# Two-layer decoder trunk on one core: a key/query scratch at one stride, and three later due times

## The chip, the cores and the metric

The kernel runs on one core of a Trainium2 chip. The metric is device microseconds of one execution. The time before is the median of three runs. Beside it stands one execution taken by the hardware profiler; all views of the profile below are of that one.

Engines are named as in the profile: PE is TensorE (PEld its weight loads), DVE is VectorE, ACT is ScalarE, POOL is GpSimd, SP is SyncE, which here issues DMAs only. A "q" behind an engine's name (ACTq, SPq) marks work of its instruction queue, DMA issues among it.

## What is computed

Two decoder layers over 1024 tokens of width 1024, all in float32, and a last norm. The parts that matter:

```python
def reference(x, norm1, w_in, b_gate, w_br, w_o, norm2, w_up, conv_w, conv_b, w_down, norm_f):
    for l in range(DEPTH):                                   # DEPTH = 2
        h = rmsnorm(x, norm1[l])
        proj = h @ w_in[l]
        qa, ka, va, qb, kb, vb, gate_pre = jnp.split(proj, splits, axis=-1)
        o_a = dilated_mixture(hd4(qa, DSW_HEADS), hd4(ka, DSW_HEADS), hd4(va, DSW_HEADS))
        o_b = stick_breaking_attention(hd4(qb, SB_HEADS), hd4(kb, SB_HEADS), hd4(vb, SB_HEADS))
        gates = jax.nn.sigmoid(gate_pre + b_gate[l])
        g_a, g_b = gates[..., :D_MODEL], gates[..., D_MODEL:]
        merged = g_a * (o_a @ w_br[l, :OUT_A]) + g_b * (o_b @ w_br[l, OUT_A:])
        x = x + merged @ w_o[l]
        up = rmsnorm(x, norm2[l]) @ w_up[l]
        a, v = up[..., :D_FF], up[..., D_FF:]
        a = causal_depthwise_conv(a, conv_w[l], conv_b[l])
        x = x + (jax.nn.gelu(a, approximate=False) * v) @ w_down[l]
    return rmsnorm(x, norm_f)
```

`dilated_mixture` is a softmax attention with ALiBi of twelve heads in three groups (window 128 at dilation 1, 512 at 4, 2048 at 16), merged by their log-sums. The groups of dilation 4 and 16 attend over tokens taken at stride 4; they are called far below, the first group near. `stick_breaking_attention` has four heads, and its weights hold a running sum over the keys.

## The kernel before

**Products.** Every float32 operand is split in a high and a low fp32r part (`split`: a cast on ACT, L129, and a subtraction on DVE, L130), and a product is three matmuls (high by high, high by low, low by high). Most projection units are a two by two blocked product done with seven block products in place of eight: `pair(...)` computes a first part alone (`ahead`, tile `r_ps`, L155 to L157) and the rest as a "seven" unit (`pair_rest.run`, tiles `i_a`, `i_c`, matmuls L887 to L889). A seven unit needs weight sums: POOL L997 and L999, DVE L1001, POOL L1004, each followed by a split of a weight piece (`w_hi` on ACT, `w_lo` on DVE). Results come back on DVE at L1013, L1018, L1026, L1031 and L1039.

**What sets the order.** PE's order is written out by hand: it is the order in which the Python code emits matmuls. The class `Dense` feeds projection units into attention. Its unit of time is a share, six matmuls of 128x512. `dense.at(n, f)` runs `f` n shares later. While one unit runs, the next is made ready by `ready`, one preparation step (one `yield` ahead of the products) at each turn; a seven unit has READY such steps. The attention items are 16 of the stick-breaking kind (B: scores `z`, a scan L627, `beta` L628, turned by `sb_t` L638), 4 of the near window (N: `p0h`, `p0l`, output L713) and 16 far ones (T, `far_item`: scores z at L584, exponent on ACT L796, turned by PE at L803 to L805, output L813). A T item starts when its key/query piece was fetched six shares ago (LEAD) and when `v1` and `v2`, the value projections of the far groups, are done. DVE, ACT, POOL and SP get their order from a scheduler that goes by priorities and estimated times in the first half of a layer, and each runs its own list strictly in order. DMAs are issued by SP, and some by ACT; every issue takes one of eight completion lanes, and waits if the lane's earlier transfer is not there yet.

**The key/query scratch.** Queries and keys of the far groups come off the projections with heads on partitions, and go through a DRAM scratch `tk` (one for each pair of heads), so that one T item can fetch its pieces as one tile `t_kq`. `pair_kq.put` casts a high part `kq_h` on ACT (L1053 for queries, L1056 for keys), takes a low part on DVE (L1054, L1057), and writes each in pieces of 64 partitions, for each of the two heads (L1062): six DMAs for a query part, four for a key part. High parts are issued by ACT, low ones by SP. `fetch_kq` (L755) reads 128 rows of 6 KB back.

**Values.** `pair_v.put` has a block of values turned by four PE transposes into bank `v_t` (L1074, one of two PSUM banks "s" that scores use as well) two shares after the block is there, and ACT L1078 and DVE L1079 split it for its own scratch. The block comes from DVE L971 (tile `rf`, in `ahead`) or from L1013 to L1039 (tile `u`, in a seven unit).

**Sums of h.** `block_sums` builds the four sums of blocks of h that seven units need (POOL L904 to L906 into `h_sum`, then a split) and spreads them over the shares: `series(after, t, f, lag, gap)` puts one quarter every `gap` steps.

Of the kernel before, what the change touches and what calls it, by code (L numbers as in the profile page):

```python
# [32 lines left out]
PT = 6  # L33
WARM = 6
GROUPS = (2, 2, 3, 4)
READY = 6
ET = mybir.EngineType
IN_ORDER = {ET.PE, ET.Activation, ET.DVE, ET.Pool}
HEAD = 4
# [13 lines left out]
def trunk_kernel(ctx, tc, x, norm1, w_in, b_gate, w_br, w_o, norm2, w_up, conv_w, conv_b, w_down, norm_f, out, depth=None, probe=None):  # L53
# [49 lines left out]
    gs = dr.tile([KD, 2, P, 2, HF], F32, name="gs")  # L103
    gd = dr.tile([NF // 2, 7, P, 2, HF], F32, name="gd")
    obd = dr.tile([P, 2, T], F32, name="obd")
    tk = [dr.tile([2, 4, P, 6, 256], F32, name=f"tk{i}") for i in range(2)]
    tv = [dr.tile([2, 4, P, 2, 256], F32, name=f"tv{i}") for i in range(2)]
    dn = [dr.tile([4, T], F32, name=f"dn{i}") for i in range(2)]
    first_half_product = {}
# [642 lines left out]
    def fetch_kq(i):  # L752

        t = R["kq", i] = sb.tile([P, 6, 256], F32R, tag="xa", bufs=4, name="t_kq")
        nc.sync.dma_start(f32(t), tk[i // 8][i // 4 % 2, i % 4])  # L755

    def fetch_v(i):
        if "vv" not in R:
# [4 lines left out]
    def far_item(dense, pr, s, r, share):  # L763
        i = 8 * pr + 4 * s + r
        slot = 2 * pr + s
        if s == 0 and r == 0:
            R["st1", pr] = sb.tile([P, 2, 2, 2, 4], F32, tag="st1", bufs=2, name="st1")
            R["ot", pr] = None
        st = R["st1", pr]
        shared = {}  # L770

        def score():
            if r == 0:
                bias = share["bias"] = sb.tile([P, 2, 256], F32, tag="bias", name="bias1")
                dve.tensor_scalar(bias[:, 0, :], base0, 4.0 * SLOPES[4 + slot], None, ALU.mult)
                dve.tensor_scalar(bias[:, 1, :], base2, 4.0 * SLOPES[8 + slot], None, ALU.mult)
            bias = share["bias"]
            pt = shared["p"] = sb.tile([P, T], F32, tag="p4", bufs=4, name="p1")
            z0, z1 = bank("s", "z10"), bank("s", "z11")
            t = R["kq", i]  # L780
            for g in range(2):
                scores(z0[:, P * g : P * g + P], t[:, 3 * g + 1, 0:P], t[:, 3 * g + 2, 0:P], t[:, 3 * g, 0:P])
            for g in range(2):
                scores(z1[:, 256 * g : 256 * g + 256], t[:, 3 * g + 1, P:256], t[:, 3 * g + 2, P:256], t[:, 3 * g, :])
            dense.scored = i + 1
            if (s, r) == (1, 0):
                near_stats(pr)
            for n in range(2):
                flat = pt[:, 256:768] if n else pt[:, 0:256]
                if n:  # L790
                    zz, pp, bb = z1, flat, bias.rearrange("p g c -> p (g c)")
                else:
                    zz, pp, bb = z0[:, 0:256].rearrange("p (g c) -> p g c", g=2), flat.rearrange("p (g c) -> p g c", g=2), bias[:, :, P:256]
                nm = st[:, 0, s, n, r : r + 1]
                dve.tensor_tensor_reduce(pp, zz, bb, 1.0, 3e38, ALU.add, ALU.min, nm)
                act.activation(flat, flat, AF.Exp, bias=nm, scale=-1.0, accum_out=st[:, 1, s, n, r : r + 1])  # L796
            if (s, r) == (1, 3):
                factors(pr)

        def turn(g):  # L800
            pt = shared["p"]
            tp = bank("t", "t1")
            pe.transpose(tp[:, 0:P], pt[:, P * g : P * g + P], ident)  # L803
            pe.transpose(tp[:, P : 2 * P], pt[:, 256 + 256 * g : 384 + 256 * g], ident)
            pe.transpose(tp[:, 2 * P : 3 * P], pt[:, 384 + 256 * g : 512 + 256 * g], ident)  # L805
            shared[g] = parts(tp, 384, "p1")

        def apply(g):
            if r % 2 == 0 and g == 0:
                share["o"] = bank("o", "o1")  # L810
            o, oc, vt = share["o"], 256 * (r % 2), R["v", i][:, g]
            for p in (0, 1):
                pe.matmul(o[:, oc : oc + 256], vt[:, 0:P], shared[g][p][:, 0:256], start=(r % 2 == 0 and g == 0 and p == 0), stop=False, skip_group_check=True)  # L813
            for p in (0, 1):
                pe.matmul(o[:, oc + P : oc + 256], vt[:, P:256], shared[g][p][:, 256:384], start=False, stop=(r % 2 == 1 and g == 1 and p == 1), skip_group_check=True)
            if g == 1:
                dense.applied = i + 1
            if r % 2 == 1 and g == 1:
                if R["ot", pr] is None:
                    R["ot", pr] = sb.tile([P, T], F32, tag="ot", name="ot")  # L820
                fold(R["ot", pr][64 * s : 64 * s + 64, 512 * (r // 2) : 512 * (r // 2) + 512], o)
                if s == 1 and r == 3:
                    join(pr)

        return [score], [(lambda g=g: turn(g), lambda g=g: apply(g)) for g in range(2)]
# [67 lines left out]
    def block_sums():  # L893


        keep = {}

        def first(t, a, b, i):
            if i == 0:
                if "r" not in keep:  # L900
                    keep["r"] = quarter("h_sum")
                new_s(t)
            r, (ah, al), (bh, bl) = keep["r"][:, i, :], a()[i], b()[i]
            pool.tensor_tensor(r, f32(al), f32(bl), ALU.subtract)  # L904
            pool.tensor_tensor(r, r, f32(ah), ALU.add)
            pool.tensor_tensor(r, r, f32(bh), ALU.subtract)  # L906

        def further(t, a, i):
            if t == 4:

                S[4] = half(0, 0)
            elif i == 0:
                new_s(t)
            r, (ah, al) = keep["r"][:, i, :], a()[i]
            dve.tensor_tensor(r, f32(ah), r, ALU.subtract)
            dve.tensor_tensor(r, r, f32(al), ALU.add)

        def in_two(t, i):
            split(*S[t][i], keep["r"][:, i, :])

        b11, b12, b21, b22 = (lambda n=n, k=k: half(n, k) for k in range(2) for n in (1, 0))
        todo = []

        def series(after, t, f, lag, gap):

            at = {}
            for i in range(4):
                at.setdefault(i * gap, []).append(lambda i=i: f(i))
                at.setdefault(i * gap + lag, []).append(lambda i=i: in_two(t, i))
            for k in range(3 * gap + lag + 1):  # L930
                todo.append((after, lambda fs=at.get(k, ()): [g() for g in fs]))

        series({"B17"}, 3, lambda i: first(3, b22, b12, i), 6, 4)
        series({"N01s"}, 1, lambda i: first(1, b12, b11, i), 6, 4)
        series({"N11s"}, 2, lambda i: further(2, b22, i), 1, 1)
        series({"plain", "01", "v0"}, 4, lambda i: further(4, b21, i), 1, 1)
        return todo

    def zeros():

        none = sb.tile([P, 4, 256], F32, tag="ot", name="none")
        pool.memset(none[0:64], 0.0)
        for pr in range(2):
            for g in range(2):
                for s in range(2):
                    nc.sync.dma_start(tk[pr][s, :, 64:128, 3 * g + 2, :].rearrange("r p c -> p r c"), none[0:64])

    def pair(dense, l, offs, tiled, put):

# [27 lines left out]
    def pair_rest(dense, l, offs, put, view, grid, kept):  # L977
# [10 lines left out]
        def run():  # L988
# [8 lines left out]
            pool.tensor_tensor(u2, a11, a21, ALU.subtract)  # L997
            yield
            pool.tensor_tensor(a21, a21, a22, ALU.add)  # L999
            yield  # L1000
            dve.tensor_tensor(a11, a21, a11, ALU.subtract)  # L1001
            w6 = piece(a11)
# [42 lines left out]
    def pair_kq(dense, l, g, pr):  # L1045
        off = 256 * g + P * pr

        def put(c, n, x, psum):
            hi = small("kq_h", F32R)
            lo = small("kq_l", F32R) if psum else x.bitcast(F32R)  # L1050
            hv, lv, xv = (t if t is x and psum else t.rearrange("p (r j) -> p r j", r=4) for t in (hi, lo, x))
            if c:
                act.mul(hv, xv, -SCALE)  # L1053
                dve.scalar_tensor_tensor(lv, xv, -SCALE, f32(hv), ALU.mult, ALU.subtract)  # L1054
            else:
                act.copy(hv, xv)  # L1056
                dve.tensor_tensor(lv, xv, f32(hv), ALU.subtract)  # L1057
            for s in range(2):
                rows = slice(64 * s, 64 * s + 64)
                for src, kind, up in ((hv, c, 0), (hv, 1, 64), (lv, 2, 0)) if c else ((hv, 0, 0), (lv, 0, 64)):  # L1060
                    there = tk[pr][s, :, up : up + 64, 3 * (g - 1) + kind, n * P : (n + 1) * P]
                    (nc.sync if src is lv else act).dma_start(there.rearrange("r p j -> p r j"), f32(src[rows]))  # L1062
            if (c, n) == (1, 1):
                dense.done.add(f"{g}{pr}")

# [2 lines left out]
    def pair_v(dense, l, g):  # L1068
# [17 lines left out]
        def put(c, n, x, psum):  # L1086
            f = x
            if psum:
                f = small("vf")
                act.copy(f.rearrange("p (r j) -> p r j", r=4), x)  # L1090
            dense.at(2, lambda: turn(c, n, f))

        off = OFF_VA + 256 * g
        return pair(dense, l, (off, off + P), True, put)
# [763 lines left out]
```

## Time and profile before

| | |
|---|---|
| median of three runs | 2773.81 us (2773.45 to 2774.67) |
| the profiled execution | 2779.93 us, of which the span of instructions is 2778.1 us |
| mean granted TensorE clock of it | 0.989 |
| busy in it: PE, PEld | 2688.1 us (97%), 2241.6 us (81%) |
| DVE, ACT, POOL | 2091.8 us (75%), 1327.2 us (48%), 695.2 us (25%) |
| moved in it | 449.92 MB, 162 GB/s |
| key/query scratch writes: of high parts from ACT | 96 of 128 KB, 3.6 us to landing |
| of low parts from SP | 64 of 128 KB, 3.4 and 3.7 us |
| key/query fetches from SP | 32 of 768 KB, 5.3 us |

In the profile's table of groups, a row has the line, the engine, the operation and its tiles, then busy time, then the idle time of the engine just before these instructions and what ended it. In the table of waits, a row says which engine waited before which tile's instruction for whom, the sum in us, how often, and the longest. In a timeline, a row has the start in us, the duration, the engine and line, and in brackets how long the engine was idle before it and what ended that. Two matmuls of 128x512 at full clock begin 0.23 us apart, though each lasts 0.39 us: they overlap.

### The profile page before, as it was taken

Reading aid. Unit: us, or ns where it says so; the run is one execution under the profiler, and the core shown is the slowest. Engines: PE = TensorE matmul, PEld = TensorE weight load, DVE = VectorE, ACT = ScalarE, POOL = GpSimd, SP = SyncE. Lnnn points to the kernel's source line nnn. Section 1 sums busy time; section 2 is a strip of 40 time slices with the busy share of each in tenths; the row PEclk is TensorE's granted clock in tenths of the full one; section 3 lists DMA queues with packets and bytes.
Section 4 is the critical chain, followed back from the end, with each engine's and each line's share of the span. In section 5 each row is a group of like instructions: output and inputs, shape, how many; then the busy total and the mean of one; then the engine's idle time right before and its main releaser. Section 6 shows DMA issues by size and latency. Waiting matters only on the chain. (4 is left out here: it accounts for less than half of the span.)

```text
span 2778.1 us, 37044 instructions
## 1 busy us (share of the span) xinstructions
PE 2688.1 (97%) x13098; PEld 2241.6 (81%) x13098; DVE 2091.8 (75%) x3132; ACT 1327.2 (48%) x2458; POOL 695.2 (25%) x509
## 2 busy tenths in 40 slices
PE   8998999999999999999999989999999999999999
PEld 8877877888888888888888778778788888888888
DVE  5877865676688888897657767556757889988965
ACT  5655633346455555532335655343544555554225
POOL 1004121213224343421110041222222334443210
PEclk9999999999999999999999989999999999999999
DMA  5023378555324434588401234876632344446863
GB/s 149 27 80 110 115 208 247 190 192 180 99 96 155 159 138 158 195 330 315 168 32 47 78 99 134 232 233 198 227 119 83 123 158 167 138 154 238 327 257 122
DMA packets 394630, 449.92 MB, mean 162 GB/s; under 512 B 22748, under 2 KB 315980, under 8 KB 392908
## 3 DMA queue, kind: packets, MB, share of 16 engines
q1 hardware_dynamic: 368332, 434.96, 47.1%
q10 hardware_dynamic: 26112, 12.59, 1.7%
q8 instruction: 104, 1.70, 0.3%
q14 instruction: 82, 0.67, 0.1%
HBM read 300.61 MB, written 146.87 MB: 161 GB/s over the span
## 5 line engine op out<-in xcount | busy, mean ns | idle before, releaser
L130 DVE TENSOR_TENSOR w_lo<-up_a,w_hi 128x512 fp32r<-128x512 f32 x240 | 236.8, 993 | 20.0 <-ACT w_hi L129 20.0
L129 ACT CAST w_hi<-up_a 128x512 fp32r<-128x512 f32 x240 | 149.4, 622 | 184.1 <-PE u_a L888 45.8
L1614 DVE TENSOR_TENSOR x<-x,d_ps 128x512 f32<-128x512 f32 (+1 forms) x228 | 152.0, 672 | 77.4 <-PE d_ps L1608 76.1
L1345 POOL TENSOR_TENSOR cv<-cv 128x512 f32<-128x512 f32 x88 | 131.8, 1508 | 249.6 <-DVE cv L1340 139.7
L129 ACT CAST w_hi<-w_raw 128x512 fp32r<-128x512 f32 x176 | 109.1, 621 | 145.0 <-PE o_ps L156 67.2
L130 DVE TENSOR_TENSOR w_lo<-w_raw,w_hi 128x512 fp32r<-128x512 f32 x176 | 127.2, 726 | 64.9 <-ACT w_hi L129 64.1
L130 DVE TENSOR_TENSOR g<-cv,g 128x512 fp32r<-128x512 f32 x154 | 151.7, 986 | 5.2 <-ACT g L129 2.8
L129 ACT CAST w_hi<-in_a 128x512 fp32r<-128x512 f32 x112 | 68.8, 617 | 136.2 <-PE i_a L888 66.1
L1606 PE MATMUL d_ps<-gd_in,w_hi 128*128 128x512 f32 (+1 forms) x340 | 130.3, 383 | 1.7 <-issue 0.9
L1608 PE MATMUL d_ps<-gd_in,w_lo 128*128 128x512 f32 (+1 forms) x340 | 129.8, 382 | 0.0
L1607 PE MATMUL d_ps<-gd_in,w_hi 128*128 128x512 f32 (+1 forms) x340 | 129.8, 382 | 0.0
L997 POOL TENSOR_TENSOR u<-in_a 128x512 f32<-128x512 f32 x28 | 37.3, 1332 | 355.3 <-DVE w_lo L130 88.1
L887 PE MATMUL u_a<-hh,w_hi 128*128 128x512 f32 x320 | 124.7, 390 | 0.3 <-DVE u L1496 0.2
L889 PE MATMUL u_a<-hh,w_lo 128*128 128x512 f32 x320 | 124.5, 389 | 0.0
L888 PE MATMUL u_a<-hl,w_hi 128*128 128x512 f32 x320 | 124.5, 389 | 0.0
L887 PE MATMUL u_a<-t_hi,w_hi 128*128 128x512 f32 x320 | 124.5, 389 | 0.0
L888 PE MATMUL u_a<-t_lo,w_hi 128*128 128x512 f32 x320 | 124.5, 389 | 0.0
L889 PE MATMUL u_a<-t_hi,w_lo 128*128 128x512 f32 x320 | 124.5, 389 | 0.0
L1606 PE MATMUL d_ps<-gd_in,wd 128*128 128x512 f32 (+1 forms) x292 | 113.9, 390 | 0.0
L129 ACT CAST g<-cv 128x512 fp32r<-128x512 f32 x154 | 94.9, 616 | 37.6 <-POOL cv L1345 29.2
L1608 PE MATMUL d_ps<-gd_in,wd 128*128 128x512 f32 (+1 forms) x292 | 112.8, 386 | 0.0
L1607 PE MATMUL d_ps<-gd_in,wd 128*128 128x512 f32 (+1 forms) x292 | 112.7, 386 | 0.0
(390 smaller groups left out, 8739.0 us busy)
## 6 DMA issues: line engine op xcount, KB each, us to landing
gd<-g SPq DMA_DIRECT2D x154, 512.0 KB, 3.6
gd_in<-gd SPq DMA_DIRECT2D x154, 512.0 KB, 6.5
up_a<-in_w_up_dram SPq DMA_DIRECT2D x80, 512.0 KB, 5.5
in_a<-in_w_in_dram SPq DMA_DIRECT2D x56, 512.0 KB, 5.0
w_raw<-in_w_in_dram SPq DMA_DIRECT2D x104, 256.0 KB, 3.0
t_kq<-tk SPq DMA_DIRECT2D x32, 768.0 KB, 5.3
wd_raw<-in_w_down_dram SPq DMA_DIRECT2D x22, 1024.0 KB, 7.9
gin<-gs SPq DMA_DIRECT2D x32, 512.0 KB, 4.3
```

The costliest lines, as they stand in the source:

```text
L129: act.copy(hi, src)
L130: dve.tensor_tensor(lo, src, f32(hi), ALU.subtract)
L887: pe.matmul(o, w[0][:, c], rh, start=(first and i == 0), stop=False, skip_group_check=True)
L888: pe.matmul(o, w[0][:, c], rl, start=False, stop=False, skip_group_check=True)
L889: pe.matmul(o, w[1][:, c], rh, start=False, stop=(last and i == 3), skip_group_check=True)
L997: pool.tensor_tensor(u2, a11, a21, ALU.subtract)
L1345: return lambda: pool.tensor_tensor(dst, a, b, ALU.subtract)
L1606: pe.matmul(o[:, sub], wh[:, c], gh[:, sub], start=(i == 0 and k in (0, 4, 5)), stop=False, skip_group_check=True)
L1607: pe.matmul(o[:, sub], wh[:, c], gl[:, sub], start=False, stop=False, skip_group_check=True)
L1608: pe.matmul(o[:, sub], wl[:, c], gh[:, sub], start=False, stop=(i == m - 1), skip_group_check=True)
L1614: dve.tensor_tensor(x, x, o[:, sub], ALU.add)
```

## The change

Four edits.

1. The scratch `tk` holds both heads' rows under one another, 128 rows of twelve 1 KB slots for each residue of the stride (six for each group: zeros, query low, query high, key high, key low, one unused). Query and key parts are written once, as one DMA of 128 partitions (256 KB) each for the high and the low part, both issued by SP. Over both layers 160 writes become 64, and ACT issues none of them. The zeros that fill the lower half of an operand are one slot per group, written once for both heads. A T item fetches with two DMAs in place of one: 64 partitions of two runs of 3 KB, and 64 partitions of six runs of 1 KB. The scores read the same operands from other slots.
2. READY goes from 6 to 7, with one empty step between POOL L999 and DVE L1001.
3. Values are turned four shares after their block, not two.
4. The first two series of `block_sums` put a quarter every five steps, not four.

```diff
-READY = 6
+READY = 7
...
-    tk = [dr.tile([2, 4, P, 6, 256], F32, name=f"tk{i}") for i in range(2)]
+    tk = [dr.tile([4, P, 12, 256], F32, name=f"tk{i}") for i in range(2)]
...
     def fetch_kq(i):
         t = R["kq", i] = sb.tile([P, 6, 256], F32R, tag="xa", bufs=4, name="t_kq")
-        nc.sync.dma_start(f32(t), tk[i // 8][i // 4 % 2, i % 4])
+        there = tk[i // 8][i % 4, 64 * (i // 4 % 2) : 64 * (i // 4 % 2) + 64]
+        nc.sync.dma_start(f32(t[0:64]).rearrange("p (g k) c -> p g (k c)", g=2), there.rearrange("p (g k) c -> p g (k c)", g=2)[:, :, 256:1024])
+        nc.sync.dma_start(f32(t[64:128]), there.rearrange("p (k b) c -> p k b c", b=2)[:, :, 0, :])
...
-        series({"B17"}, 3, lambda i: first(3, b22, b12, i), 6, 4)
-        series({"N01s"}, 1, lambda i: first(1, b12, b11, i), 6, 4)
+        series({"B17"}, 3, lambda i: first(3, b22, b12, i), 6, 5)
+        series({"N01s"}, 1, lambda i: first(1, b12, b11, i), 6, 5)
...
     def zeros():
-        pool.memset(none[0:64], 0.0)
+        pool.memset(none, 0.0)
         for pr in range(2):
             for g in range(2):
-                for s in range(2):
-                    nc.sync.dma_start(tk[pr][s, :, 64:128, 3 * g + 2, :].rearrange("r p c -> p r c"), none[0:64])
+                nc.sync.dma_start(tk[pr][:, :, 6 * g, :].rearrange("r p c -> p r c"), none)
...
             pool.tensor_tensor(a21, a21, a22, ALU.add)
+            yield
             yield
             dve.tensor_tensor(a11, a21, a11, ALU.subtract)
...
-            for s in range(2):
-                rows = slice(64 * s, 64 * s + 64)
-                for src, kind, up in ((hv, c, 0), (hv, 1, 64), (lv, 2, 0)) if c else ((hv, 0, 0), (lv, 0, 64)):
-                    there = tk[pr][s, :, up : up + 64, 3 * (g - 1) + kind, n * P : (n + 1) * P]
-                    (nc.sync if src is lv else act).dma_start(there.rearrange("r p j -> p r j"), f32(src[rows]))
+            for src, kind in ((hv, 2), (lv, 1)) if c else ((hv, 3), (lv, 4)):
+                there = tk[pr][:, :, 6 * (g - 1) + kind, n * P : (n + 1) * P]
+                nc.sync.dma_start(there.rearrange("r p j -> p r j"), f32(src))
...
-            dense.at(2, lambda: turn(c, n, f))
+            dense.at(4, lambda: turn(c, n, f))
```

Three places show how instructions move. The first is PE, in the stick-breaking stretch of the first layer, at the first value turn. Before:

```order
L155 MATMUL r_ps<-hh_362,w_hi 128x512
L156 MATMUL r_ps<-hl_363,w_hi 128x512
L157 MATMUL r_ps<-hh_362,w_lo 128x512
L1074 MATMUL v_t<-ident,rf 128x128 x4
L584 MATMUL z<-kt,qt 128x512
L585 MATMUL z<-kt,ql 128x512
```

Now, from those scores on:

```order
L584 MATMUL z<-kt,qt 128x512
L585 MATMUL z<-kt,ql 128x512
L155 MATMUL r_ps<-hh_362,w_hi 128x512
L156 MATMUL r_ps<-hl_363,w_hi 128x512
L157 MATMUL r_ps<-hh_362,w_lo 128x512
L649 MATMUL sb_o<-sbh,vb 128x256
L638 MATMUL sb_t<-ident,beta 128x128 x3
L156 MATMUL r_ps<-hl_363,w_hi 128x512
L157 MATMUL r_ps<-hh_362,w_lo 128x512
L1074 MATMUL v_t<-ident,rf 128x128 x4
L649 MATMUL sb_o<-sbh,vb 128x256
```

The turn `v_t` now stands behind twelve more matmuls of the projection (two shares; rows that repeat are left out), and with them behind two pairs of scores, a piece of the stick-breaking output and a turn of `beta`.

The second place is ACT, at the end of the last key/query unit of a layer, where the second pair of T items of a head pair begins (`p` is the tile of far scores, `st` its statistics, lines after the change are two higher). Before:

```order
L1056 CAST kq_h<-u 128x512
L129 CAST w_hi<-u 128x512
L1062 DMA tk_91<-kq_h 64x4x128 x2
L1053 ACTIVATE kq_h<-u 128x512
L129 CAST w_hi<-in_a 128x512
L1062 DMA tk_91<-kq_h 64x4x128 x4
L796 ACTIVATE p_4452,st_4221<-p_4452,st_4221 128x256
L796 ACTIVATE p_4452,st_4221<-p_4452,st_4221 128x512
```

Now:

```order
L129 CAST w_hi<-u 128x512
L1058 CAST kq_h<-u 128x512
L599 COPY fold<-o_4297 64x512
L129 CAST w_hi<-in_a 128x512
L1055 ACTIVATE kq_h<-u 128x512
L129 CAST w_hi<-in_a 128x512
L798 ACTIVATE p_4427,st_4206<-p_4427,st_4206 128x256
L798 ACTIVATE p_4427,st_4206<-p_4427,st_4206 128x512
```

The six DMA rows between the casts and the exponents are gone.

The third place is DVE, in a value unit of the first layer, around the weight difference L1001 (L1003 after the change) and the results L1018 and L1026 (L1020 and L1028). Before:

```order
L1013 TENSOR_TENSOR u<-u,i_a 128x512
L130 TENSOR_TENSOR w_lo<-in_a,w_hi 128x512
L1018 TENSOR_TENSOR u_3964<-u,i_c 128x512
L130 TENSOR_TENSOR w_lo<-in_a,w_hi 128x512
L1001 TENSOR_TENSOR in_a<-in_a 128x512
L1026 TENSOR_TENSOR u_3964<-u_3964,i_a 128x512
```

Now:

```order
L1015 TENSOR_TENSOR u<-u,i_a 128x512
L130 TENSOR_TENSOR w_lo<-in_a,w_hi 128x512
L1020 TENSOR_TENSOR u_3932<-u,i_c 128x512
L1003 TENSOR_TENSOR in_a<-in_a 128x512
L130 TENSOR_TENSOR w_lo<-in_a,w_hi 128x512
L1028 TENSOR_TENSOR u_3932<-u_3932,i_a 128x512
```

The weight difference still stands ahead of L1028; a low part that stood ahead of it now stands behind it.

More of the change, by code (lines that the diff above doesn't have):

```diff
@@ L781, in score @@
             for g in range(2):
-                scores(z0[:, P * g : P * g + P], t[:, 3 * g + 1, 0:P], t[:, 3 * g + 2, 0:P], t[:, 3 * g, 0:P])
+                scores(z0[:, P * g : P * g + P], t[:, 3 * g + 1, 0:P], t[:, 3 * g, 0:P], t[:, 3 * g + 2, 0:P])
             for g in range(2):
-                scores(z1[:, 256 * g : 256 * g + 256], t[:, 3 * g + 1, P:256], t[:, 3 * g + 2, P:256], t[:, 3 * g, :])
+                scores(z1[:, 256 * g : 256 * g + 256], t[:, 3 * g + 1, P:256], t[:, 3 * g, P:256], t[:, 3 * g + 2, :])
             dense.scored = i + 1
```

## The prediction

> **What bounds the kernel now.** I read the page's busy table first, then the windows of 50 us, then who PE waits for.
>
> ```profile
> span 2778.1 us, 37044 instructions
> PE 2688.1 (97%) x13098; PEld 2241.6 (81%) x13098; DVE 2091.8 (75%) x3132; ACT 1327.2 (48%) x2458; POOL 695.2 (25%) x509
> 250.00:300.00 50.00, 43.59 (x213) 35.97 (x212) 35.79 (x63) 27.09 (x59) 31.23 (x23) 0.90 0.29 91
> 400.00:450.00 50.00, 45.12 (x216) 36.03 (x216) 31.02 (x63) 18.65 (x39) 9.39 (x7) 0.97 0.91 256
> 1600.00:1650.00 50.00, 44.01 (x222) 36.88 (x223) 31.35 (x64) 24.93 (x61) 27.26 (x21) 0.88 0.30 97
> ```
>
> PE is the bound: 2688.1 of 2778.1 us. The change takes no matmul away, so it can win only from the 90 us in which PE stands, and from the clock: in the windows (PE's busy time is first, the granted clock third from the end) a stretch with stops has a clock of 0.88 to 0.97. Both losses sit in the attention part of each layer. The table of waits says whom PE waits for:
>
> ```profile
> PE sb_t L638 <- DVE beta L628: 10.8, 12, 2.2
> PE o L713 <- ACT p0h L129: 6.4, 2, 3.2
> PE o L813 <- ACT p1h L129: 5.4, 5, 1.6
> PE v_t L1074 <- DVE rf L971: 5.3, 2, 2.7
> PE t L803 <- ACT p L796: 5.2, 3, 2.2
> PE v_t L1074 <- DVE u L1026: 5.1, 2, 3.0
> PE o L813 <- DVE p1l L130: 4.7, 10, 1.1
> PE z L584 <- DVE st L795: 4.3, 4, 1.8
> PE i_a L887 <- ACT w_hi L129: 2.6, 2, 1.6
> PE t L804 <- ACT p L796: 1.8, 5, 0.4
> PE i_a L887 <- DVE u L1031: 1.5, 2, 0.8
> ```
>
> Three are close to the change: both value turns (5.3 and 5.1 us) and the far probabilities `p` (5.2 and 1.8). A stop costs more than itself, as the first value turn in PE's timeline shows, with DVE's rows below:
>
> ```profile
> 221.67 0.39 PE L156 MATMUL r_ps<-hl,w_hi 128*128 128x512 f32 x1
> 221.90 0.40 PE L157 MATMUL r_ps<-hh,w_lo 128*128 128x512 f32 x1
> 224.97 0.63 PE L1074 MATMUL v_t<-ident,rf 128*128 128x128 f32 x4 [2.67 <-DVE rf L971]
> 227.24 0.53 PE L584 MATMUL z<-kt,qt 128*128 128x512 f32 x1 [1.18 <-ACT stay L625]
> 228.00 0.63 PE L155 MATMUL r_ps<-hh,w_hi 128*128 128x512 f32 x1
> 228.43 0.63 PE L156 MATMUL r_ps<-hl,w_hi 128*128 128x512 f32 x1
> 223.14 1.09 DVE L628 TENSOR_TENSOR beta<-beta,stay 128x895 f32<-128x895 f32 x1
> 224.15 0.68 DVE L971 TENSOR_TENSOR rf<-q1s,r_ps 128x512 f32<-128x512 f32 x1
> ```
>
> Ahead of the stop matmuls begin 0.23 us apart, behind it 0.43: half speed, for some seven of them, so 7 x 0.20 = 1.4 us lost on top of the wait. I take 1.4 us for each stop that is removed or made.
>
> **The change part by part.**
>
> *Value turns two shares later, first place* (`v_t` from `rf`, once a layer). Removed: the wait, 5.3 us in both layers; the wait behind it (1.18, in both layers 2.4), since `v_t` takes one of the two banks that `z` needs; two slow stretches, 2.8. Together 10.5. After the change PE goes on at 222.13 with the four scores (0.9), two shares (2.8), outputs and turn (0.8), so it reaches `v_t` at about 226.6; `rf` is done at 224.83. Late next is `sb_t`, which needs `beta` (done at 224.23): PE would be there at 222.13 + 0.9 + 1.4 + 0.5 = 224.9, so with 0.7 us to spare. The bank is still shared, and `v_t` now stands close ahead of the next scores: I allow 2 us of new waits a layer for it and credit **6.5 us** (bounds 0 and 10.5).
>
> *Value turns, second place* (`v_t` from `u` of L1026, once a layer), and *ACT without DMA issues*. These belong together; the rows are ACT, POOL, DVE and PE around the last key/query unit ahead of the values:
>
> ```profile
> 390.40 4.41 ACTq L1062 DMA_DIRECT2D tk<-kq_h  x4
> 394.85 0.62 ACT L129 CAST w_hi<-in_a 128x512 fp32r<-128x512 f32 x1 [3.97 <-DMA tk<-kq_h]
> 396.38 1.28 POOL L997 TENSOR_TENSOR u<-in_a 128x512 f32<-128x512 f32 x1 [10.08 <-DVE w_lo L130]
> 397.74 1.26 POOL L999 TENSOR_TENSOR in_a<-in_a 128x512 f32<-128x512 f32 x1
> 399.03 0.69 DVE L1001 TENSOR_TENSOR in_a<-in_a 128x512 f32<-128x512 f32 x1 [2.83 <-POOL in_a L999]
> 399.64 0.68 DVE L1026 TENSOR_TENSOR u<-u,i_a 128x512 f32<-128x512 f32 x1
> 400.38 0.66 PE L1074 MATMUL v_t<-ident,u 128*128 128x128 f32 x4 [3.02 <-DVE u L1026]
> ```
>
> One chain: four issues hold ACT's queue for 4.41 us, the cast `w_hi` starts when they are through, its low part releases POOL L997, L999 follows, L1001 waits for it, and L1026, which is ready, stands behind L1001. Moving the turn alone gains one share, not two: the fifth product accumulates in the bank that L1026 reads, and begins one share behind the turn's old place. So alone it gives 2 x 1.4 = 2.8. With the issues off ACT the chain starts up to 4 us earlier, and the rest of the 3.0 goes too. All of it is 5.1 + 2.8 of slow clock = 7.9; I credit **6.5** (bounds 2.8 and 7.9).
>
> *Far exponents behind ACT's issues.*
>
> ```profile
> 447.09 0.69 DVE L795 CUSTOM_DVE_ANT_0 p<-z,bias 128x512 f32<-128x512 f32 x1
> 447.52 3.97 ACTq L1062 DMA_DIRECT2D tk<-kq_h  x4
> 451.55 0.51 ACT L796 ACTIVATE p<-p,st 128x256 f32<-128x256 f32 x1 [3.54 <-issue]
> 452.20 0.33 PE L803 MATMUL t<-ident,p 128*128 128x128 f32 x1 [2.23 <-ACT p L796]
> ```
>
> `p` is there at 447.78, ACT comes to it at 451.55: the 3.97 us of four issues lie between, and nothing else. Without them the exponents (some 1.2 us) end by 449.1; PE asked for them at 452.20 - 2.23 = 449.97. So the waits for `p` go: 5.2 + 1.8 in the table, plus 1.4 for each layer's long one, 9.8. I credit **8** (bounds 5 and 9.8), since DVE's rows of L795 may come later in a new order.
>
> *The prepared weight piece* (`i_a` for `w_hi` and for L1031, 2.6 + 1.5 = 4.1): the same chain over POOL L997, whose tile comes free when scratch writes have landed. Credit **2.5** (bounds 0 and 4.1). *Scores behind statistics* (`z` for L795, 4.3): only their two at key/query units are touched; credit **1** (bounds 0 and 3.6).
>
> *Weight difference later, READY 7.* In the listed order L1001 still stands ahead of L1026, with one `w_lo` less ahead of it. In feed-forward units the extra step is empty. I credit nothing; if L1001 stays the head of DVE's list at the wrong time, the price is that of the chain above, inside its bounds. *Sums of h five steps apart*: POOL's list is the same and so is ACT's around it; nothing. The wait it could have touched, `o` for `p0h` (6.4), stays, and so does most of `beta` (10.8).
>
> *The DMAs.*
>
> ```profile
> t_kq<-tk SPq DMA_DIRECT2D x32, 768.0 KB, 5.3
> DMA to landing us min/median/max: 4.2/5.3/10.9
> tk<-kq_h ACTq DMA_DIRECT2D x96, 128.0 KB, 3.6
> 427.14 0.56 SPq L755 DMA_DIRECT2D t_kq<-tk  x1
> 444.35 0.22 PE L584 MATMUL z<-t_kq 128*128 128x128 f32 x1
> ```
>
> (The second row is of those fetches.) SP keeps its 64 scratch writes; one of each pair now waits for ACT's cast, which comes ahead of the low part that the other waits for, so SP's list waits for nothing later than before. It gains 32 fetches. A fetch is asked for 17.2 us ahead of its use and lands after 5.3: 11.9 us of cover, and even twice 5.3 costs nothing. The issues themselves, 32 of 0.56 us, are 18 us over both layers on an engine that does nothing else.
>
> The row above has ACT held for 4.41 us by four issues, about 1.1 us each, where SP's took 0.56. [...] The trace shows ACT, not SP, as the queue that holds up PE.
>
> *New waits.* `v1` and `v2` are done two shares later, so all 32 far items start later against the dense work and meet other neighbours. Their waits now (5.4 + 4.7 + 4.3 = 14.4 us) are 0.45 an item. I allow four new stops of 1.4 us each, slow clock or wait, that is **-5.5** (bounds 0 and -15, where every item waits twice as long as now).
>
> Sum: 6.5 + 6.5 + 8 + 2.5 + 1 - 5.5 = **19 us**. The profiled execution took 2779.93 us (its span and 1.8 around it), which becomes 2761; it stands 6.1 above the median of 2773.81, which becomes **2755 us**.
>
> **The rivals.**
>
> *The stops only move* (no change). Each waiting instruction still has its chain behind DVE, at 75% busy; the far items start elsewhere. For it: the row of `o` for `p1l`, ten small waits that have nothing to do with the change. Against it: ACT is 48% busy and the 4 us of issues have no second cause. It would need new waits of 19 to 30 us against credits of 24.5: 2768 to 2779; I take 2772.
>
> *The split fetch comes late* (slower). Half of each fetch now comes in 1 KB runs, 384 of them, and the fetches of the first items of a layer go out while the DMA engines are busy for 0.91 of the time (window 400 to 450). The worst fetch took 10.9 us with its 6 KB runs. If a small run costs so much that such a fetch takes twice that, 21.8, it is 4.6 us past its use; it decides from 17.2 us on. Four such items a layer are 8 x 4.6 = 37 us, more than the credits of 24.5: 2786. Behind a late fetch the next DMAs of SP's list wait as well, since completion lanes are handed on in turn. Against it: the median of 5.3, and 4 MB less written at that very time.
>
> *The clock doesn't come back with the gaps.* If half speed comes from something else than the stop ahead of it, six stops give back 6 x 1.4 = 8.4 us less: 10.6 in place of 19, 2763. The rows at 221.90 to 228.43 speak against it. [...]
>
> *The edit doesn't do what it says.* For the weight difference and the sums of h the listed order says so already; it is in the sum at nothing.
>
> *All of it gains*: 10.5 + 7.9 + 9.8 + 4.1 + 3.6 = 36 and no new wait: 2738.
>
> **How the numbers follow.** My forecast, with part of the credits: 0.52. The clock stays: 0.08. All of it gains: 0.13. The stops only move: 0.15, of which a third is still faster by more than the bound below. The split fetch late: 0.12. The range runs from 2736, just past the full gain, to 2771; beyond it lie the slower rival and half of the case of no change, about 0.2 together. Without the far cases the forecast's own range is 2745 to 2764. What a measurement of this kernel can tell from no change is about 0.2%, 5.5 us: faster means under 2768.3, slower over 2779.4. Faster 0.52 + 0.08 + 0.13 + 0.05 = 0.78, same 0.1, slower 0.12.
>
> **What would show it.** In the changed profile the rows of ACTq with `tk` are gone, and `t` for `p` falls from 7.0 us in two rows to under 1.5. `v_t` for `rf` and for L1026 are gone or under 1 us together. ACT's wait for DMA `tk` ahead of `w_hi` is gone. The clock rises from 0.989 to about 0.993. `o` for `p0h` stays at 6.4. The prediction is wrong if PE's sum of stops stays near 90 us, with new rows that name a fetch `t_kq`, a load of `in_a` or `z` behind `v_t`.

## The result, and the profile after

| | before | changed |
|---|---|---|
| median | 2773.63 us (4 runs, 2772.07 to 2774.67) | 2749.56 us (4 runs, 2745.2 to 2750.43) |
| ratio | | 0.9911, 95% interval 0.9893 to 0.9928 |
| profiled execution, its span | 2779.93, 2778.1 us | 2750.43, 2748.6 us |
| clock | 0.989 | 0.993 |

The kernel became 24 us faster; 19 were forecast, inside the range. Beside the experiments below the changed kernel ran once more, with a median of 2748.78 us and a ratio of 0.9906 (0.9892 to 0.9921).

The page and rows of PE's table of waits of the changed kernel (who waits for whom, total us, times, longest; rows on which no reading rests are left out):

```profile
span 2748.6 us, 36975 instructions
PE 2672.8 (97%) x13098; PEld 2232.0 (81%) x13098; DVE 2096.1 (76%) x3132; ACT 1328.1 (48%) x2458; POOL 694.2 (25%) x509
PE sb_t L638 <- DVE beta L628: 14.5, 12, 2.2
PE z L584 <- DVE st L797: 8.0, 11, 1.3
PE o L713 <- ACT p0h L129: 6.4, 2, 3.2
PE o L815 <- DVE p1l L130: 6.1, 7, 1.8
PE br_ps L155 <- ACT br_w L129: 3.1, 1, 3.1
PE br_ps L157 <- DVE br_w L130: 2.3, 1, 2.3
PE z L584 <- ACT stay L625: 2.1, 3, 1.2
PE i_a L889 <- DVE u L1028: 1.4, 2, 1.2
PE o L815 <- ACT p1h L129: 0.5, 2, 0.3
```

Both rows of `v_t` are gone, and so are both rows of `t` waiting for ACT's `p` (5.2 and 1.8 us before). The wait of `z` for `stay` behind the first value turn fell from 4.5 to 2.1, and `o` for `p1h` from 5.4 to 0.5. The other signs that the prediction named are there too: the clock is 0.993, `o` for `p0h` stays at 6.4, and the span without PE's busy time is 75.8 us in place of 90.0. PE's busy time fell by 2688.1 - 2672.8 = 15.3 us with the same 13098 matmuls. Most of it is the clock: of the 29.5 us between the two profiled executions about half is standing time and half is matmuls that took less time, up to 13.7 us of it by the count of slow spans below. The stops in the timelines sum to 82.3 us before and 68.2 now. The trace's record of the granted clock has PE, up to its last matmul, at half clock for 61.4 us before (18 spans of 3.41 us, in 15 stretches) and 34.1 us now (10 spans, in 7 stretches). An estimate from these: with matmuls 0.43 us apart in place of 0.23, a span that is worked through loses at most half of itself, 1.7 us, so eight spans fewer are worth up to 13.7 us.

New or longer are `sb_t` for `beta` (10.8 to 14.5), `z` for L797 (4.3 to 8.0), `o` for `p1l` (4.7 to 6.1), and two waits for `br_w`, 5.4 us together (1.4 before).

Where the time came from can be read by taking the same dense matmul (the k-th of tile `r_ps`, or of `i_a` and `i_c`) in both timelines and subtracting its start. The steps of that difference, in us (first and second layer; negative is earlier now):

| stretch | first | second |
|---|---|---|
| stick-breaking items, with the first value turn | -4.2 | -3.5 |
| near items | -0.1 | -1.5 |
| key/query units up to the second value turn | -2.6 | -3.0 |
| across the second value turn | -3.9 | -4.0 |
| far items | -4.9 | -6.3 |
| branch projections behind them | +1.3 | +5.4 |

These sum to -27.3; 1.9 more lie at the program's start, where input transposes wait for no cause that the profile shows, and the feed-forward parts give 0.5. The profiled execution before stood 6 us above its median, the one after 1, so the medians differ by 5 us less.

The rows that answer to the first value turn, of the changed kernel (PE, then DVE):

```profile
222.65 0.60 PE L1074 MATMUL v_t<-ident,rf 128*128 128x128 f32 x4
227.68 0.90 PE L638 MATMUL sb_t<-ident,beta 128*128 128x128 f32 x3 [2.00 <-DVE beta L628]
223.16 2.29 DVE L627 TENSOR_TENSOR_SCAN stay<-stay,zero 128x1024 f32<-128x1024 f32 x1 [1.15 <-ACT stay L625]
226.41 1.22 DVE L628 TENSOR_TENSOR beta<-beta,stay 128x1023 f32<-128x1023 f32 x1
```

The turn itself no longer waits. PE now comes sooner to the next `sb_t` and waits 2.0 us there for the last and longest scan (2.29 us) and the `beta` behind it.

Second value turn and far exponents (PE, ACT, PE):

```profile
391.14 0.47 PE L889 MATMUL i_a<-hh,w_hi 128*128 128x512 f32 x1 [1.23 <-DVE u L1028]
392.61 0.60 PE L1074 MATMUL v_t<-ident,u 128*128 128x128 f32 x4
410.64 0.63 ACT L1055 ACTIVATE kq_h<-u 128x512 fp32r<-128x512 f32 x1 [0.27 <-DVE u L1041]
412.38 0.51 ACT L798 ACTIVATE p<-p,st 128x256 f32<-128x256 f32 x1 [1.11 <-DVE st L797]
414.31 0.27 PE L805 MATMUL t<-ident,p 128*128 128x128 f32 x1
```

As worked out, `i_a` now stands in front of the turn and waits for the bank that L1028 (L1026 before) reads: 1.23 us here, 0.16 in the second layer, in place of 3.02 and 2.10. Between the cast `kq_h` and the exponent ACT waits only for DVE's statistics (1.11 us), where four issues stood before, and PE's turn of `p` comes without a wait.

The transfers of the scratch in the changed kernel, and one row of experiment 3 (KB each, median us to landing):

```profile
t_kq<-tk SPq DMA_DIRECT2D x64, 384.0 KB, 6.9
tk<-kq_h SPq DMA_DIRECT2D x32, 256.0 KB, 2.4
tk<-u SPq DMA_DIRECT2D x24, 256.0 KB, 3.2
...
tk<-kq_h SPq DMA_DIRECT2D x96, 128.0 KB, 2.5
```

A write of 256 KB over 128 partitions lands in 2.4 to 3.2 us, one of 128 KB over 64 took 3.4 to 3.7. The shape is not shown to be the reason: in experiment 3, where SP issues all the old pieces, these land in 2.5 us too (last row). Half a fetch takes 6.9, where the whole took 5.3. No wait of PE's scores is put down to `t_kq`.

### The profile page after: what moved, and what is told of

Same layout as the page of the kernel before. It is cut to its first block, busy times and chain, and to the rows that moved or that the text cites. A ratio compares the mean times of both kernels' runs of the same rounds, so it can differ in the third digit from the quotient of the medians.

```text
span 2748.6 us, 36975 instructions
## 1 busy us (share of the span) xinstructions
PE 2672.8 (97%) x13098; PEld 2232.0 (81%) x13098; DVE 2096.1 (76%) x3132; ACT 1328.1 (48%) x2458; POOL 694.2 (25%) x509
```

## The experiments

All ratios are against the kernel before on the same chip; intervals are 95%.

**1. The scratch edit alone.** The `tk`, `fetch_kq`, `zeros` and `put` parts of the diff; the rest as before.

> Only the scratch edit of the change; value turns after two shares, READY 6 and gap 4 as before. My theory: the gain from ACT's freed queue is in this edit, that is 8 (far exponents) + 2.5 + 1 + the part of the second value turn that hangs on ACT's cast (7.9 - 2.8 = 5): 12 to 17 us faster than before, 2757 to 2762. Rival, the later value turns carry the change and the far items' new place does the rest: at most 5 us faster. In the trace PE's wait t for ACT p goes in my theory, and the first value turn's wait for rf (5.3 us) stays.

2753.54 us (2752.81 to 2757.67), ratio 0.9928 (0.9915 to 0.9941): 20 us faster, more than I allowed for. In its table of waits the `p` rows are gone, and the value turns are still there:

```profile
PE v_t L1073 <- DVE rf L972: 4.8, 2, 2.4
PE v_t L1073 <- DVE u L1027: 3.9, 2, 2.5
```

The scratch edit carries most of the change. The second turn's wait fell only from 5.1 to 3.9, so not the part I had put down to ACT's cast, but the far items, made the surplus over my sum. Taken matmul by matmul as above, the two layers gain 2.8 us at the second turn, 5.0 in the key/query units and 15.2 at the far items, where my sum had 5, 2.5 and 9.

**2. The value turns alone.**

```diff
-            dense.at(2, lambda: turn(c, n, f))
+            dense.at(4, lambda: turn(c, n, f))
```

> Only the value turns at four shares; scratch, READY and gap as before. My theory: 6.5 for the turn of rf and 2.8 for that of u, less new waits of the far items, which now begin later: 3 to 9 us faster, 2765 to 2771; ACT's four issues still hold up the far exponents somewhere. Rival, the turns carry the change: 15 us or more. Second rival, the stops only move: within 2 us of before.

2767.97 us (2764.15 to 2770.91, 11 runs), ratio 0.9977 (0.9968 to 0.9985): 6 us faster, as my theory had it. The stop for `p` is still there, in one of 3.2 us a layer, and `sb_t` has the same new wait as in the changed kernel:

```profile
PE sb_t L638 <- DVE beta L628: 14.2, 14, 2.2
PE t L803 <- ACT p L796: 6.4, 2, 3.2
```

**3. Issues off ACT, in the old pieces.**

```diff
-                    (nc.sync if src is lv else act).dma_start(there.rearrange("r p j -> p r j"), f32(src[rows]))
+                    nc.sync.dma_start(there.rearrange("r p j -> p r j"), f32(src[rows]))
```

> The kernel before with one word changed: the high parts' writes, in their old pieces, are issued by SP too (160 small writes, all on SP). My theory, it is ACT's queue that costs: 8 to 15 us faster than before, 2759 to 2766, a little less than the scratch edit alone since SP's list is longer by 96 issues. Rival, it is the number of writes and their landing (POOL's tiles come free late): within 3 us of before. Second rival, SP becomes the head of line: slower than before.

2771.83 us (2766.43 to 2775.41, 12 runs), ratio 0.9990 (0.9981 to 0.9998): 2 us. My theory fell, as it was put: freeing ACT is not enough. The trace shows what takes its place (SP, POOL, DVE, PE in the first layer):

```profile
417.30 4.98 SPq L1062 DMA_DIRECT2D tk<-kq_h  x2
434.12 0.32 SPq L996 DMA_DIRECT2D u<-q  x1
434.29 1.29 POOL L997 TENSOR_TENSOR u<-in_a 128x512 f32<-128x512 f32 x1 [21.06 <-DMA tk<-u]
436.99 0.69 DVE L1001 TENSOR_TENSOR in_a<-in_a 128x512 f32<-128x512 f32 x1 [1.51 <-POOL in_a L999]
441.85 0.41 DVE L795 CUSTOM_DVE_ANT_1 p<-z,bias 128x256 f32<-128x256 f32 x1
442.32 0.48 PE L584 MATMUL z<-t_kq 128*128 128x128 f32 x1 [3.92 <-DVE st L795]
```

From 417.3 to 432 SP issues nothing but small scratch writes. The load of the next unit's `u` comes behind them at 434.12, POOL starts on that unit's tile at 434.29, the weight difference and its splits follow on DVE, the statistics L795 stand behind these, and PE waits 3.92 us for them. So the stop for `p` has become a stop of `z` for L795 (10.0 us in the run, 4.3 before): SP became the head of line.

**4. Few writes, but the high parts from ACT.** The changed kernel with one line back:

```diff
-                nc.sync.dma_start(there.rearrange("r p j -> p r j"), f32(src))
+                (nc.sync if src is lv else act).dma_start(there.rearrange("r p j -> p r j"), f32(src))
```

> The changed kernel, with the 32 writes of the high parts (256 KB, 128 partitions) issued by ACT again; all else as changed (2750 us). Theory A, it takes both to be few and off ACT's queue, and each issue from ACT still waits for a completion lane in front of casts: 2 to 6 us slower than the changed kernel, 2752 to 2756. Theory B, only the number of writes matters (moving 160 small ones to SP alone gave 2 us): within 2 us of it. Theory C, any issue from ACT costs as much as the four did: 8 us or more slower.

2753.84 us (2751.45 to 2755.32), ratio 0.9927 (0.9914 to 0.9939): 4 to 5 us slower than the changed kernel (2749.56 and 2748.78), theory A in size, though the intervals of the ratios overlap. On the same chip ran the changed kernel without its empty step (experiment 5, 2747.28 to 2749.23): all five runs here (2751.45 and up) lie above all four there. Its trace (ACT, then PE):

```profile
1790.01 0.62 ACT L1058 CAST kq_h<-u 128x512 fp32r<-128x512 f32 x1 [5.21 <-DMA tk<-kq_h]
1790.66 0.37 ACTq L1062 DMA_DIRECT2D tk<-kq_h  x1
1795.94 0.33 PE L584 MATMUL z<-t_kq 128*128 128x128 f32 x1 [4.22 <-DVE st L797]
```

An issue from ACT takes 0.37 us here (the old pieces' took 0.64 by their median), so it is not the issuing that costs. A cast stood still for 5.21 us until an earlier scratch write had landed, and PE then waited 4.22 us. By these two runs most of the scratch edit's 20 us comes with the merged writes. The issuing engine is worth 2 us with the old pieces and 4 to 5 with the merged ones. What it is in the merging that pays, the number of writes, their width, the 4 MB less that are moved or the split fetch, no run here separates.

**5. READY 7 and the empty step alone, and left out.** Alone on the kernel before:

> Only READY 7 and the empty step ahead of the weight difference. My theory: nothing, within 3 us of before, since the difference still stands ahead of the same result in DVE's list. Rival: that result comes off the head-of-line wait and the second value turn's wait goes: 5 to 8 us faster.

2772.97 us (2768.71 to 2777.34, 11 runs), ratio 0.9995 (0.9987 to 1.0004): nothing. Left out of the changed kernel (READY 6, one `yield` less):

> The changed kernel with READY 6 and without the empty step ahead of the weight difference. My theory, the step does nothing: within 2 us of the changed kernel's 2750. Rival, it keeps the weight difference off the head of VectorE's list once the rest is in place: 4 us or more slower, with waits of i_a for L1026 and for w_hi.

2748.94 us (2747.28 to 2749.23), ratio 0.9908 (0.9895 to 0.9922): nothing either.

**6. The sums of h at gap 4 in the changed kernel.**

> The changed kernel with the sums of h at gap 4, as before. My theory, the gap does nothing: within 2 us of the changed kernel's 2750. Rival, it spares the near window's waits: 3 us or more slower, with the wait of o for p0h over 6.4 us.

2745.47 us (2744.46 to 2746.63), ratio 0.9897 (0.9884 to 0.9911). This hinted at 3 to 4 us that the wider gap costs, though its waits were the same as the changed kernel's (`p0h` 6.4 in both). So I left both small edits out together, beside the changed kernel on one chip:

> Only the scratch edit and the value turns at four shares: READY 6 and gap 4 as before. My theory, the other two edits do nothing: within 2 us of the changed kernel on the same chip. Rival, the wider gap costs 4 us, as the run without it hinted (2745.5): 3 us or more faster than the changed kernel.

> The changed kernel itself once more, beside the three below on the same chip, so that they are compared with it there. Expected 2747 to 2751.

2748.69 us (2747.86 to 2749.82) against 2748.78 (2744.96 to 2751.54): the same. So the two edits together do nothing. Whether gap 4 with READY 7 is really 3 us faster stays open: its four runs lie below the four of experiment 5's second kernel on the same chip, but the intervals of the ratios overlap, and it was not run again.

**7. The value turns at two shares in the changed kernel.**

> The changed kernel with the value turns at two shares again (all other edits in). My theory, the first place's wait for rf (2.4 and 2.4 us, with slow clock and the bank's 1.2 behind it) comes back and the new wait of sb_t for beta goes: 3 to 7 us slower than the changed kernel, close to the scratch edit alone (2753.5). Rival, the turns' gain of 6 us alone is gone once ACT's queue is free: within 2 us of the changed kernel.

2751.1 us (2748.83 to 2752.76), ratio 0.9915 (0.9900 to 0.9930), against 0.9906 (0.9892 to 0.9921) for the changed kernel on the same chip: 2.3 us, not clear of the spread, nearer the rival than my theory. The waits of the turns come back, and others go:

```profile
PE sb_t L638 <- DVE beta L628: 10.5, 10, 2.2
PE v_t L1074 <- DVE rf L972: 4.8, 2, 2.4
PE o L815 <- DVE p1l L130: 3.3, 6, 1.1
PE v_t L1074 <- DVE u L1028: 2.8, 2, 1.4
```

`sb_t` is back at 10.5, `o` for `p1l` at 3.3, `z` for L797 at 2.9, and `br_w` waits 1.4. Against these, `o` for `p1h` is back at 4.3 and `z` for `stay` at 4.5. On top of the scratch edit, turning values two shares later takes 7.6 us of waits off the turns and 6 off `p1h` and `stay`, and gives it back at the other four places: the stops sum to 65.7 us here and to 65.9 in the changed kernel's second profile. On other chips the scratch edit alone and with the turns (experiment 6) have ratios 6 us apart, so 2 to 6 us is what these runs show of the turns' worth there.

**8. The value turns at three shares in the changed kernel.**

> The changed kernel with the value turns at three shares. By the chain at the first place: rf is done some 0.4 us after PE gets there, and the turn stands ahead of sb_t, so that beta's new wait of 2.0 us shrinks by the turn's place and no more: within 3 us of the changed kernel, 2745 to 2752. Rival, three is as bad as two: 2753.

2741.77 us (2739.76 to 2743.71), ratio 0.9880 (0.9863 to 0.9896): 7 us faster than the changed kernel on the same chip, past what I expected, and the best of all kernels here. The intervals of the two ratios just touch (0.9896 and 0.9892), and no run of the one lies among the runs of the other.

```profile
PE sb_t L638 <- DVE beta L628: 12.5, 12, 2.2
PE z L584 <- DVE st L797: 5.2, 11, 1.3
PE br_ps L155 <- DVE gin L1259: 4.1, 3, 2.7
PE o L815 <- DVE p1l L130: 1.3, 5, 0.4
```

The turns wait no longer, as at four, but the far items begin only one share later, and `o` for `p1l` falls from 6.1 to 1.3. Matmul by matmul, the far items of both layers together gain 15 us, where they gained 11 in the changed kernel. The branch projections of the second layer lose 4 us here too, now for `gin` (2.7 us at once). What the wait for `p1l` was in the changed kernel can be read from POOL, DVE and PE in the first layer:

```profile
439.07 1.28 POOL L998 TENSOR_TENSOR u<-in_a 128x512 f32<-128x512 f32 x1 [12.32 <-DMA tk<-u]
441.74 0.69 DVE L1003 TENSOR_TENSOR in_a<-in_a 128x512 f32<-128x512 f32 x1 [4.26 <-POOL in_a L1000]
442.35 0.55 DVE L130 TENSOR_TENSOR p1l<-t,p1h 128x384 fp32r<-128x384 f32 x1
442.95 0.39 PE L815 MATMUL o<-p1l,t_v 128*128 128x256 f32 x1 [1.79 <-DVE p1l L130]
```

The weight difference L1003, the very one that was asked for later, is the head of DVE's list for 4.26 us until POOL is through, and the low part of the far probabilities stands behind it. This is one of seven such waits, and that its going makes the 4 us is an argument from the rows, not tried by itself.

**9. The splits of the sums asked for later.** The changed kernel with

```diff
-        series({"B17"}, 3, lambda i: first(3, b22, b12, i), 6, 5)
-        series({"N01s"}, 1, lambda i: first(1, b12, b11, i), 6, 5)
+        series({"B17"}, 3, lambda i: first(3, b22, b12, i), 8, 5)
+        series({"N01s"}, 1, lambda i: first(1, b12, b11, i), 8, 5)
```

> The changed kernel with the split of each sum of h asked for eight steps behind its sum, not six, in the first two series. In ACT's list the casts t_hi, which wait for POOL's sums, then stand behind the near window's casts p0h. Theory: the wait of o for p0h (3.2 us in each layer, with 1.2 to 1.7 of slow clock behind each) goes: 5 to 9 us faster than the changed kernel, 2741 to 2745. Rival, DVE's low parts or the later splits wait in its place: within 2 us of it.

2748.94 us (2745.45 to 2750.07), ratio 0.9907 (0.9892 to 0.9922): the rival. The stop left the place where it was (262 us) and came back behind it (278 us):

```profile
PE o L713 <- DVE p0l L130: 10.2, 12, 2.5
PE o L713 <- ACT p0h L129: 5.8, 2, 2.9
```

## Why the prediction was right, point by point

- *PE bounds, and a stop costs itself and about 1.4 us of clock.* Right, and it is half of the gain: up to 13.7 us of slow clock went with 14.1 us of stops. The 1.4 us is no fixed price: in the traces matmuls at half speed, up to 1.7 us lost in a span of 3.41, came behind some stops and not behind others (last section). The rival in which the clock stays would have left PE's busy time as it was.
- *First value turn, 6.5 credited.* -4.2 and -3.5, 7.7 in all. The stop that replaces it is that of the tile named, `sb_t` for `beta`, at 2.0 us a layer, though not at the turn of `beta` for which 0.7 us to spare were worked out, but at the next one, behind the longest scan.
- *Second value turn, 6.5 credited.* -3.9 and -4.0, 7.9: the upper bound. The wait of `i_a` for the bank is there as worked out.
- *Prepared weight piece, 2.5 credited.* -2.6 and -3.0, 5.6 over the key/query units, more than the bound of 4.1. The named stops are gone; where the other 1.5 us came from was not traced.
- *Far exponents and scores, 8 + 1 credited, less 5.5 for new waits.* The far items gave 11.2 net of their new waits, and the waits for `p` went to nothing. The later start also took `o` for `p1h` from 5.4 to 0.5, which the sum did not hold; it is 0.7 with the turns alone (experiment 2) and 4.3 with the scratch edit alone. New waits came, as `z` for L797 and `o` for `p1l`, but the larger loss was placed wrongly. It came behind the far items, at the branch projections: +1.3 and +5.4, 6.7 against an allowance of 5.5 at the far items. Rows of the changed kernel's ACT there, second layer:

```profile
1962.77 0.62 ACT L129 CAST w_hi<-w_raw 128x512 fp32r<-128x512 f32 x1 [5.33 <-DMA w_raw<-in_w_o_dram]
1966.37 1.13 ACT L129 CAST br_w<-br_raw 128x512 fp32r<-128x512 f32 x2
1967.56 0.50 PE L155 MATMUL br_ps<-oh_a,br_w 128*128 128x512 f32 x1 [3.10 <-ACT br_w L129]
```

  ACT's list puts a cast for the next projection, whose weights are not there yet, ahead of the cast that PE needs: 5.33 us at the head of line. Every run above with turns at four shares whose waits were read has this wait for ACT (1.7 to 3.5 us); in those with two or three shares it is missing, or 0.4 us. At three shares the wait for `gin` stands in its place, so a cure for the cast alone may not win the loss back; none was tried.
- *Why the scratch edit gains* is the step that was only half right. The text put it on ACT's queue and let SP's longer list pass, because it waits for nothing later than before. That holds for 64 merged writes; with 160 on SP the list itself became the wait (experiment 3). Merging the writes was the larger part. The text also read 1.1 us for each issue from ACT out of a row of four; by the median one took 0.64, and one from SP 0.59. Issued all from SP, the writes were 2 us faster with the old pieces (experiment 3) and 4 to 5 with the merged ones (experiment 4).
- *Split fetch late*: no. A half lands in 6.9 us by the median, 1.6 more than the whole did, and in 10.2 at most, which is inside the 17.2 us between asking and use.
- *READY, the empty step and the gap at nothing*: right for READY and the empty step, alone and left out, and for all three left out together. The gap by itself stays open (experiment 6).
- *What no term held*: 1.6 us in the near items and 1.9 at the program's start came without a cause in the prediction. That part of the gain is luck, and so is some of the agreement of the sum: four of its terms came out larger than credited, and a loss that it had not named took part of that back.

## What to carry to other kernels

Moving the DMA issues off ACT alone was worth 2 us here (experiment 3), as the list they went to was itself waited for; with the writes merged as well it was 20 (experiment 1). So merge the writes first, then move them, and follow what stands behind them in the new list. A due time has a best value, not a direction: here the turn at three shares (2741.8 us) beat two (2751.1) and four (2748.8), as every share also moves the items that hang on it past the head of another engine's list. Price a TensorE stop with the slow clock behind it (here 14.1 us of stops went with up to 13.7 us of slow clock), and count the lists' heads (here L1003, L627 and a cast that waits for its weights) as what is late next.

## What the runs showed of the hardware

Over the fourteen profiled executions of this study I counted the stops of PE that have no other within 8 us, and looked whether matmuls at half speed follow within 5 us. Of 373 stops under 1.3 us one is followed by them, of 51 from 1.3 to 1.6 us 8 are, of 18 from 1.6 to 2.1 us 9, and of 36 above that 31. Length alone did not decide. The profile of the changed kernel has both kinds, before the same turn in the two layers (PE, then windows with PE's busy time first and the granted clock third from the end):

```profile
183.73 0.55 PE L638 MATMUL sb_t<-ident,beta 128*128 128x128 f32 x3 [2.20 <-DVE beta L628]
1544.72 0.55 PE L638 MATMUL sb_t<-ident,beta 128*128 128x128 f32 x3 [2.17 <-DVE beta L628]
179.85:183.26 3.41, 1.68 (x9) 1.23 (x8) 3.41 (x3) 3.05 (x6) 0.00 (x0) 1.00 0.20 59
183.26:186.68 3.42, 2.95 (x16) 2.57 (x17) 3.38 (x7) 2.11 (x6) 0.00 (x0) 1.00 0.26 75
1541.77:1545.18 3.41, 1.24 (x10) 0.97 (x9) 3.41 (x4) 2.13 (x4) 0.00 (x0) 1.00 0.00 0
1545.18:1548.60 3.42, 3.42 (x12) 2.85 (x12) 3.14 (x7) 2.04 (x6) 0.00 (x0) 0.50 0.26 77
```

Behind 2.20 us of standing the matmuls begin 0.23 us apart, behind 2.17 they begin 0.43 apart. The clock's record shows what differs. In all fourteen traces the granted clock was 0.5 or 1.0, and every stretch between two changes was a whole multiple of 3.41 us, to within 3 ns (in the changed kernel's trace from 3.41 us, one multiple, to 1215.15 us, 356 of them). I cut each execution at these multiples; the windows above are four of the pieces. The stop of 2.20 us lies across two windows, 1.73 and 0.47 us; the one of 2.17 lies in one window, and the clock of the next is 0.5. Counted over all windows at full clock in the fourteen traces, without the first 20 us and the last 15, the next window was at half clock in none of 10737 in which PE stood less than 1.3 us, in 44 of 111 with 1.3 to 1.9 us, and in all 88 with more (none of 1534, 7 of 17 and all 15 in the two traces of the kernel before and the changed one). What decides between 1.3 and 1.9 us is not shown.

The first of these windows started 2.29 us after the program's first instruction in the profiled execution before, 2.36 us in the changed kernel's, and from 0.2 to 2.8 us after it over all fourteen. By these starts one and the same stop could be cut in two in one execution and not in the next, and a span of half clock, by the estimate above up to 1.7 us lost, could come or go. That is the size of the differences that the small edits left undecided, but no run shows that it made them, or the spread between runs.
